# Storing the first of four output units in four column pieces instead of one DMA

## Chip, cores, metric

One core of a Trainium2 chip. The metric is the device time of one execution in microseconds (us), median of several runs. The profile's span is about 1.75 us shorter than that time (82.8 for 84.5).

## The reference, cut to what matters

Rotary embedding on an array of 8 x 8 heads, 1024 positions, 64 columns, single precision: 16.8 MB in, 16.8 MB out.

```
angles = np.outer(positions * scale, freqs)
cos, sin = np.cos(angles), np.sin(angles)
out_first  = x_first * cos - x_second * sin
out_second = x_first * sin + x_second * cos
```

## The kernel before

The array is cut into four units of 128 partitions x 8192 columns (4 MB in single precision, 32 KB per row). GpSimd issues the loads of units 1 to 3, which cast to half precision on the way. VectorE computes each half of a unit, ScalarE copies it to a single-precision output buffer. The kernel before stores units 0 and 1 whole, from GpSimd's queue; units 2 and 3 go out in halves, from SyncE's queue.

```
xout = ctx.enter_context(tc.tile_pool(name="xout", bufs=3))
...
pin(nc.gpsimd.dma_start(out=Xf[0][:, :NH], in_=xv[0][:, :NH]))
...
for u in range(1, NU):
    pin(nc.gpsimd.dma_start(out=Xf[u], in_=xv[u]))
...                                     # tables of sine and cosine: cut
for u in range(NU):
    OUT = xout.tile([P, N], FP32, tag="O")
    for s in range(2):
        ...                             # four VectorE instructions: cut
        pin(nc.scalar.copy(out=OUT[:, ns], in_=Xf[u][:, ns]))
        if u >= NU // 2:
            pin(nc.sync.dma_start(out=ov[u][:, ns], in_=OUT[:, ns]))
    if u < NU // 2:
        pin(nc.gpsimd.dma_start(out=ov[u], in_=OUT))
```

Of the kernel before, what the change touches and what calls it, by code (L numbers as in the profile page):

```python
# [21 lines left out]
def kernel(  # L22
# [8 lines left out]
    nc = tc.nc  # L31
    pin = tc.keep_in_program_order
# [8 lines left out]
    N = K * D  # L41
# [11 lines left out]
    ov = out.rearrange("b h s d -> (b h s d)").rearrange("(u p n) -> u p n", p=P, n=N)  # L53
# [34 lines left out]
        out=one, in_=one, compare_op=ALU.not_equal, fill=1.0, base=0,  # L88
        pattern=[[-1, G], [-G, HP]], channel_multiplier=1,
    ))  # L90
    for u in range(1, NU):
# [9 lines left out]
        out=posf, in_=pos_i64.bitcast(I32).rearrange("p (k t) -> p k t", t=2)[:, :, 0]  # L101
# [3 lines left out]
        out=y,  # L105
# [8 lines left out]
        out=r, in0=m, scalar=_MAGIC, in1=y, op0=ALU.subtract, op1=ALU.subtract  # L114
# [5 lines left out]
        out=ra.bitcast(I32), in0=r.bitcast(I32), scalar1=0x7FFFFFFF, scalar2=None, op0=ALU.bitwise_and  # L120
# [5 lines left out]
    for g in range(0, G, 2):  # L126
        ps = spread.tile([P, 2, 2, W], FP32, tag="g")
        for i in range(2):
            nc.tensor.matmul(  # L129
                out=ps[:, i].rearrange("p t w -> p (t w)"),  # L130
# [12 lines left out]
# [3 lines that stand above are left out]
            ks = slice(s * KH, (s + 1) * KH)  # L146
            ns = slice(s * NH, (s + 1) * NH)
            Xs = X[u][:, ks]
            sin_b = T[:, 0, ks].unsqueeze(2).broadcast_to((P, KH, 2, half))
            cos_b = T[:, 1, ks].unsqueeze(2).broadcast_to((P, KH, 2, half))  # L150
            pr = tmp.tile([P, KH, 2, half], FP16, tag="pr")
            pin(nc.vector.tensor_tensor(out=pr, in0=Xs, in1=sin_b, op=ALU.mult))  # L152
            pin(nc.vector.tensor_tensor(out=Xs, in0=Xs, in1=cos_b, op=ALU.mult))  # L153
            pin(nc.vector.tensor_tensor(  # L154
                out=Xs[:, :, 0, :], in0=Xs[:, :, 0, :], in1=pr[:, :, 1, :], op=ALU.subtract
            ))
            pin(nc.vector.tensor_tensor(  # L157
                out=Xs[:, :, 1, :], in0=pr[:, :, 0, :], in1=Xs[:, :, 1, :], op=ALU.add
            ))
            pin(nc.scalar.copy(out=OUT[:, ns], in_=Xf[u][:, ns]))  # L160
            if u >= NU // 2:
                pin(nc.sync.dma_start(out=ov[u][:, ns], in_=OUT[:, ns]))
        if u < NU // 2:
            pin(nc.gpsimd.dma_start(out=ov[u], in_=OUT))  # L164


# [33 lines left out]
```

## Time and profile before

| | before |
|---|---|
| time, median (range) | 84.51 us (84.47 to 84.59) |
| span of the profile | 82.8 us |
| VectorE busy | 60.3 us (73%) |
| ScalarE busy | 40.1 us (49%) |
| HBM traffic | 33.6 MB, 406 GB/s over the span |

The page's part on DMA queues (columns: packets, MB, share of 16 engines' span) says how the traffic is split. q0 is GpSimd's queue, q1 SyncE's, q10 ScalarE's:

```profile
q0 software_dynamic: 864, 15.73, 66.4%
q1 hardware_dynamic: 720, 9.44, 27.2%
```

The shares of the queues (with 3.2% for q10) add to 97%: the 16 DMA engines have work nearly all the time. VectorE at 73% works early and stops 13 us before the end. The prediction reads the rows that show this. Beside the views, it and this document use the trace's record of single DMA packets (start, queue, bytes, duration); tables of those are in ordinary fences. A packet is one stretch of work of one of the 16 engines. Every large DMA ends on each engine with a completion packet of 4 bytes; the DMA has landed when the semaphore that it counts up is full. The period of packets is the time from one start to the next on one engine, and a ring is what one queue has in store for one engine. The record doesn't name the engine, so periods rest on linking each packet to the one that starts where it ends.

### The profile page before, as it was taken

The numbers are of one execution on the slowest core, as the hardware profiler recorded it, in microseconds if no ns is written. First come the engines' busy times: TensorE is split into PE (matmuls) and PEld (weight loads), VectorE is DVE, ScalarE is ACT, GpSimd is POOL, SyncE is SP. The second block draws the span as 40 slices with busy tenths as digits, with TensorE's granted clock in tenths as the row PEclk, the third lists the DMA queues.
The fourth block names the chain that finished last, engine by engine and source line by source line (L and its number), as shares of the span: only waits on it lengthen the run. The fifth ranks groups of instructions, "written<-read, shape, count | busy, mean of one in ns | idle before, by whom it ended". The sixth has DMA issues, their size and how long they took to land.

```text
span 82.8 us, 179 instructions
## 1 busy us (share of the span) xinstructions
PE 7.0 (8%) x18; PEld 2.7 (3%) x18; DVE 60.3 (73%) x40; ACT 40.1 (49%) x18; POOL 4.6 (6%) x14
## 2 busy tenths in 40 slices
PE   0011799200000000000000000000000000000000
PEld 0011233000000000000000000000000000000000
DVE  0306276999999999999999999999999997000000
ACT  0602159999960690294088049209606912950000
POOL 4920000000000002000000200000000000000000
PEclk9999999975555555555555555555555555555555
DMA  2899998997999899699979989999899999999991
GB/s 40 335 326 269 293 333 182 253 238 150 246 253 198 182 253 238 143 253 253 127 301 459 507 348 412 507 443 420 380 436 420 412 420 436 444 420 436 428 428 55
DMA packets 1874, 26.22 MB, mean 317 GB/s; under 512 B 338, under 2 KB 338, under 8 KB 338
## 3 DMA queue, kind: packets, MB, share of 16 engines
q0 software_dynamic: 864, 15.73, 66.4%
q1 hardware_dynamic: 720, 9.44, 27.2%
q10 hardware_dynamic: 290, 1.06, 3.2%
HBM read 16.79 MB, written 16.78 MB: 406 GB/s over the span
## 4 chain that ended last, share of the span: by engine, by line
DVE 55%; ACT 14%; issue 6%; DMA 6%; PE 5%; DVEq 1%; ACTq 0%
DVE pr L152 19%; DVE X L153 19%; DVE X L157 9%; DVE X L154 6%; DMA freq_row<-in_freqs_dram 6%; ACT T L139 5%; ACT OUT L160 4%; PE ps L129 4%; ACT X L140 4%; DVEq L195 1%; PE cfreq L97 1%; ACT tab L122 1%; DVE r L113 1%; DVE y L104 1%; ACTq L69 0%
## 5 line engine op out<-in xcount | busy, mean ns | idle before, releaser
L160 ACT CAST OUT<-X 128x4096 f32<-128x4096 f16 x8 | 28.8, 3606 | 24.2 <-DVE X L157 24.2
L152 DVE TENSOR_TENSOR pr<-X,T 128x4096 f16<-128x4096 f16 x8 | 18.3, 2292 | 1.0 <-ACT T L139 0.7
L153 DVE TENSOR_TENSOR X<-X,T 128x4096 f16<-128x4096 f16 x8 | 18.3, 2292 | 0.3
L154 DVE TENSOR_TENSOR X<-X,pr 128x2048 f16<-128x2048 f16 x8 | 9.8, 1225 | 0.3
L157 DVE TENSOR_TENSOR X<-pr,X 128x2048 f16<-128x2048 f16 x8 | 9.7, 1219 | 0.0
L139 ACT CAST T<-ps 128x1024 f16<-128x1024 f32 x6 | 5.7, 1030 | 2.6 <-PE ps L129 2.6
L129 PE MATMUL ps<-tab,sel 128*128 128x512 f16 x16 | 6.4, 584 | 2.2 <-ACT tab L122 2.2
L137 DVE CAST T<-ps 128x1024 f16<-128x1024 f32 x2 | 2.5, 1225 | 2.2 <-PE ps L129 2.2
L140 ACT CAST X<-X0f 128x4096 f16<-128x4096 f32 x1 | 3.7, 3651 | 0.0
L164 POOL DMA_DIRECT2D out_dram<-OUT x2 | 1.1, 536 | 40.3 <-ACT OUT L160 40.3
L95 DVE COPY sel<-one 128x2048 f16<-128x2048 f16 x1 | 0.7, 693 | 2.8 <-POOL one L87 2.8
L117 ACT ACTIVATE tab<-r 128x256 f16<-128x256 f32 x1 | 0.4, 416 | 4.3 <-DVE r L113 4.3
L129 PEld LDWEIGHTS <-sel 128*128 128x128 f16 x16 | 2.2, 138 | 6.0 <-issue 5.8
L117 ACT ACT_TABLE_LOAD x1 | 1.3, 1283 | 2.1 <-issue 2.1
L92 POOL DMA_DIRECT2D X<-in_x_dram x3 | 2.0, 658 | 0.0
L100 DVE CAST posf<-pos_i 128x8 f32<-128x8 int32 x1 | 0.2, 172 | 2.3 <-DMA pos_i<-in_positions_dram 2.3
L97 PE MATMUL cfreq<-freq_row,coef 1*128 1x32 f32 x2 | 0.6, 392 | 5.9 <-DMA freq_row<-in_freqs_dram 5.9
L104 DVE TENSOR_TENSOR y<-posf,cfreq 128x256 f32<-128x256 f32 x1 | 0.4, 422 | 0.5 <-PE cfreq L97 0.5
L83 POOL DMA_DIRECT2D X<-in_x_dram x1 | 0.7, 667 | 0.8 <-POOLq L181 0.8
L97 PEld LDWEIGHTS cfreq<-freq_row,coef 1*128 1x128 f32 x2 | 0.5, 305 | 5.8 <-issue 5.8
L122 ACT ACTIVATE tab<-ra,quarter 128x256 f16<-128x256 f32 x1 | 0.5, 507 | 0.0
L113 DVE SCALAR_TENSOR_TENSOR r<-m,y 128x256 f32<-128x256 f32 x1 | 0.4, 424 | 0.0
(10 smaller groups left out, 1.9 us busy)
## 6 DMA issues: line engine op xcount, KB each, us to landing
out_dram<-OUT POOLq DMA_DIRECT2D x2, 4096.0 KB, 20.8
out_dram<-OUT SPq DMA_DIRECT2D x4, 2048.0 KB, 11.6
X<-in_x_dram POOLq DMA_DIRECT2D x3, 2048.0 KB, 28.7
X0f<-in_x_dram SPq DMA_DIRECT2D x1, 1024.0 KB, 4.8
X<-in_x_dram POOLq DMA_DIRECT2D x1, 1024.0 KB, 11.7
X0f<-in_x_dram ACTq DMA_DIRECT2D x1, 1024.0 KB, 12.2
pos_i<-in_positions_dram ACTq DMA_DIRECT2D x1, 8.0 KB, 5.0
freq_row<-in_freqs_dram ACTq DMA_DIRECT2D x1, 0.1 KB
```

The lines of the kernel that those rows point to most:

```text
L92: pin(nc.gpsimd.dma_start(out=Xf[u], in_=xv[u]))
L97: nc.tensor.matmul(out=cfreq, lhsT=coef, rhs=freq_row, start=True, stop=True)
L117: pin(nc.scalar.activation(out=tab[:, 0], in_=r, func=AF.Sin, bias=0.0, scale=-_TWO_PI_DN))
L129: nc.tensor.matmul(out=ps[:, i].rearrange("p t w -> p (t w)"), lhsT=sel[:, g + i].rearrange("s h q -> s (h q)"), rhs=tab.rearrange("s t k ...
L137: pin(nc.vector.tensor_copy(out=dst, in_=ps))
L139: pin(nc.scalar.copy(out=dst, in_=ps))
L140: pin(nc.scalar.copy(out=Xf[0][:, NH:], in_=X0f[:, :NH]))
L152: pin(nc.vector.tensor_tensor(out=pr, in0=Xs, in1=sin_b, op=ALU.mult))
L153: pin(nc.vector.tensor_tensor(out=Xs, in0=Xs, in1=cos_b, op=ALU.mult))
L154: pin(nc.vector.tensor_tensor(out=Xs[:, :, 0, :], in0=Xs[:, :, 0, :], in1=pr[:, :, 1, :], op=ALU.subtract))
L157: pin(nc.vector.tensor_tensor(out=Xs[:, :, 1, :], in0=pr[:, :, 0, :], in1=Xs[:, :, 1, :], op=ALU.add))
L160: pin(nc.scalar.copy(out=OUT[:, ns], in_=Xf[u][:, ns]))
```

## The change

Unit 0 is stored in four DMAs of 2048 columns (1 MB each, rows of 8 KB). As the quarters lie within one half each, the first two can be issued as soon as the first half is ready. The intent is to start the first store earlier, in smaller pieces.

```diff
         if u < NU // 2:
-            pin(nc.gpsimd.dma_start(out=ov[u], in_=OUT))
+            parts = 4 if u == 0 else 1
+            for i in range(parts):
+                c = slice(i * N // parts, (i + 1) * N // parts)
+                pin(nc.gpsimd.dma_start(out=ov[u][:, c], in_=OUT[:, c]))
```

## The prediction

> **What bounds the kernel now.** I read the page's slices first, then the table of DMA issues, then a table of stretches, and last the chain.
>
> The row of slices (each slice is 82.8 / 40 = 2.07 us):
>
> ```profile
> DVE  0306276999999999999999999999999997000000
> ACT  0602159999960690294088049209606912950000
> POOL 4920000000000002000000200000000000000000
> ...
> DMA  2899998997999899699979989999899999999991
> ...
> HBM read 16.79 MB, written 16.78 MB: 406 GB/s over the span
> ```
>
> VectorE is full from slice 7 to slice 33 and then stops; the DMA row is full from slice 2 to slice 39 and is still full in the five or six slices in which no engine computes. That is the first sign that the data movement sets the end. The stretches make it firm (columns: stretch, its length, busy time and count of PE, PEld, DVE, ACT, POOL, the granted clock, the DMA share, GB/s):
>
> ```profile
> 32.00:42.00 10.00, 0.00 (x0) 0.00 (x0) 9.83 (x8) 3.95 (x2) 0.06 (x1) 0.50 0.95 184
> 42.00:52.00 10.00, 0.00 (x0) 0.00 (x0) 9.86 (x6) 6.56 (x2) 0.53 (x1) 0.50 1.02 439
> 52.00:62.00 10.00, 0.00 (x0) 0.00 (x0) 9.86 (x7) 3.92 (x2) 0.00 (x0) 0.50 1.00 431
> 62.00:72.00 10.00, 0.00 (x0) 0.00 (x0) 7.71 (x5) 5.76 (x2) 0.00 (x0) 0.50 0.99 423
> 72.00:80.00 8.00, 0.00 (x0) 0.00 (x0) 0.00 (x0) 1.45 (x1) 0.00 (x0) 0.50 1.00 428
> ```
>
> The DMA share is 0.95 to 1.02 in each stretch. The rate jumps at 42 us because loads cast to half precision and the view counts the bytes that arrive: 184 GB/s of half precision is 368 GB/s read in this stretch. After 42 us it is stores alone, near 430 GB/s to the end.
>
> Third, when each store is issued and lands (KB each, us from issue to landing; the first two lines come from views of the stretches around each issue, the third from the one around the last store):
>
> ```profile
> out_dram<-OUT POOLq DMA_DIRECT2D x1, 4096.0 KB, 21.2
> ...
> out_dram<-OUT POOLq DMA_DIRECT2D x1, 4096.0 KB, 20.4
> ...
> out_dram<-OUT SPq DMA_DIRECT2D x1, 2048.0 KB, 8.4
> ```
>
> Unit 0's store is issued at 31.52 us and lands 21.2 us later, at 52.7. The trace's record of single DMA packets shows its first packet at 42.05 us: it spends 10.5 us waiting behind the loads, which share GpSimd's queue (q0), and 9.7 us moving. The last store, from SyncE, is issued at 73.45 and lands 8.4 us later, though it holds 2 MB, which takes 4.86 us to move (first packet 76.36, completion packets from 80.87 on). So it too queues, for nearly 3 us, behind stores issued before it.
>
> The chain of waits must be read against this. It says
>
> ```profile
> DVE 55%; ACT 14%; issue 6%; DMA 6%; PE 5%; DVEq 1%; ACTq 0%
> ```
>
> and ends with the last ScalarE copy (69.84 to 73.44 us). It follows semaphores and doesn't see transfers queue behind each other. From 42 us on the engines have work without a pause, so any DMA time added to unit 0's store moves every later packet and the end.
>
> **What the Trainium skill says.** (1) "DMA: Bandwidth & Descriptors", section "Why small descriptors are slow (HBM only)": each packet carries a fixed overhead of about 3 cycles on the engine's inner bus, against 32 bytes per cycle of data. The trace agrees in size, see below. (2) The same page, "Anatomy of one DMA", puts a fixed cost near 2.0 us on each DMA, mostly completion latency. The trace shows that such latency isn't paid by the next DMA in the queue: on one engine the completion packet of unit 0's store starts at 51.734 us and the first data packet of unit 1's at 51.740. (3) "Queues, rings and completion order": an engine takes descriptors in ring order and goes round the queues packet by packet. The trace agrees: unit 0's store begins only when the third load is through (its completion packets at 42.04 to 42.67 us), and when SyncE's first store joins unit 1's, 16 KB and 32 KB packets alternate with a period of 1.816 us, the sum of one of each.
>
> **The change part by part.**
>
> *Issue.* The order of instructions shows that GpSimd's four quarters no longer all wait for both ScalarE copies: the first two need only the first (ends at 24.0 us), the last two the second (31.2 us). Four issues at 0.54 us each cost GpSimd 4 x 0.54 = 2.1 us in place of 0.54; it has nothing else to do there (it waited 26.8 us before this store). So half of the unit is issued some 7 us earlier. It brings nothing: the ring is in order, and the third load fills it until 42 us in either case.
>
> *Data packets.* A row of unit 0 is now four packets of 8 KB in place of one of 32 KB. I take the period from one packet's start to the next on one engine:
> - 32 KB, unit 0's store alone: 1209.5 ns (median).
> - 16 KB, the last stores, alone: 607 ns.
> - A straight line through both: 1209.5 - 607 = 602.5 ns for 16 KB, so 301.25 ns for 8 KB, and 607 - 602.5 = 4.5 ns fixed per packet. An 8 KB packet should take 305.75 ns.
> - Check: the first load has 8 KB packets, with a 64-byte packet of the positions between them; period 313 ns, the small packet takes 7 ns of it, so 306 ns. (The skill's 3 cycles, at 32 bytes per cycle and 27.1 bytes per ns, i.e. 32768 / 1209.5, are an estimate of 3.5 ns: the same size.)
>
> Per row: 4 x 305.75 - 1209.5 = 13.5 ns. Each engine has 128 / 16 = 8 rows: 8 x 13.5 = 0.108 us.
>
> *Completion packets.* Three DMAs more, each with one completion packet per engine. They are recorded with 9 ns and set the next data packet back by 6: 3 x 6 to 9 = 0.02 to 0.03 us.
>
> *Waits.* Unit 3's first output copy reuses unit 0's buffer and must now wait for four stores. It starts at 62.84 us, released by VectorE; unit 0's store lands at 52.7 and would land at 52.8. 10 us of slack, so nothing. Unit 1's store (45.56 us) gets a wait on a semaphore reused from the first load, which landed before 13 us: nothing.
>
> *VectorE, ScalarE.* No instruction is changed. VectorE has about 2 us of slack before the last store would come late to its engines (issued at 73.45, first packet 76.36; the first load shows about 1.0 us from issue to first packet).
>
> Sum: 0.11 + 0.02 = 0.13 us on the DMA engines, all of it passed to the end because they are full until 81.5 us. 84.51 + 0.13 = 84.64 us, or +0.15%.
>
> **The rivals.**
>
> *A fixed cost per DMA is paid in series.* If each of three added DMAs cost the skill's 2.0 us, the time would be 84.5 + 6 = 90.5 us. Against it speak the 6 ns between two DMAs of one ring above, and the same at the load-to-store boundary.
>
> *An earlier start pays.* If quarters issued at 24 us could slip in between the loads, or if the first half landed early, it would matter only if it freed work or filled idle DMA time. The DMA share has no hole between 5 and 81 us, and the loads it would displace would be late by as much. Worth 0 to -0.3 us; and a later load might then stop VectorE: unit 3's data lands at 43 us and is needed at 55.75, so 12 us of slack hides even that.
>
> *Descriptor writing on GpSimd is slow beside VectorE, or the ring fills.* GpSimd's four issues fall beside VectorE's 2.3 us multiplies. The before shows 0.53 to 0.54 us for each such issue beside VectorE, so no sign of a clash; even a doubling ends before 35 us, 7 us ahead of need. A ring too small for 3 more sets of descriptors would hold GpSimd up until loads drain, and this could leave a hole at 42 us. Nothing shows a limit; if it struck I would expect under 1 us.
>
> *Shorter HBM runs cost more.* Each quarter writes 8 KB at a pitch of 32 KB. SyncE's stores already write 16 KB at that pitch at the full rate (607 ns); the first load reads 8 KB at it, also full. For writes of 8 KB there is no direct evidence. At a 5% loss: 0.05 x 9.7 = 0.5 us, 85.0 us.
>
> **Range and chances.** The three timed runs before span 84.47 to 84.59, so the effect is about the size of their spread. Downward I allow 0.15 us of noise or a better joint between loads and stores, upward 0.3 us for the HBM and ring rivals: 84.4 to 84.9. Leaving the 2% band needs 1.7 us, over ten times my sum; only the first or third rival, which the trace speaks against, gives it. Within 2%: 0.96; slower 0.025; faster 0.015.
>
> **What the profile after would show.** q0 has 3 x 128 = 384 data packets more and 3 x 16 = 48 completion packets more, so 864 + 432 = 1296 packets and the same 15.73 MB. 8 KB store packets run at about 306 ns from 42.05 us to about 51.87 (before: 51.74). GpSimd's issues start near 24 and 31.5 us. The last landing moves from 81.86 to about 82.0 us, and VectorE and ScalarE keep their starts within 0.1 us. The prediction is wrong if 8 KB packets are longer than 320 ns, if there is a pause between the quarters, if store packets show up before the loads end, or if the end doesn't follow the DMA engines.

## The result, and the profile after

84.69 us median (84.53 to 84.73, six runs) against 84.51 (six runs). The ratio is 1.0016 with a 95% interval of 1.0003 to 1.0029: slower, and clear of noise, by 0.03% to 0.29%. Ratios here are the mean time of one kernel's runs over that of the other's of the same rounds, so not quite the ratio of the quoted medians. A second set of six runs (below) gave 1.0025. The prediction was 84.64 us, with a range of 84.4 to 84.9.

The page's slices of the kernel after (tenths busy in 40 slices), then its line of q0:

```profile
DVE  0306376999999999999999999999999995000000
...
POOL 4920000000031005000001100000000000000000
...
DMA  2899997997999799799969999989999899999990
```

```profile
q0 software_dynamic: 1296, 15.73, 66.5%
```

GpSimd now has issues in slices 12 and 13, 7 us ahead of the ones in slice 16, but the DMA row is as full as before and of the same shape. q0 has 1296 packets in place of 864 for the same bytes, and its share of the engines' time grew by 0.1% of the span.

GpSimd's timeline of the kernel after (start, us, engine, line, operation, count, idle time before and what ended it), and where its transfers land (from views of the stretches around each issue; KB each, us from issue to landing):

```profile
24.11 1.08 POOL L167 DMA_DIRECT2D out_dram<-OUT  x2 [19.45 <-ACT OUT L160]
31.33 1.05 POOL L167 DMA_DIRECT2D out_dram<-OUT  x2 [6.13 <-ACT OUT L160]
45.37 0.53 POOL L167 DMA_DIRECT2D out_dram<-OUT  x1 [12.98 <-ACT OUT L160]
```

```profile
out_dram<-OUT POOLq DMA_DIRECT2D x2, 1024.0 KB, 22.4
...
out_dram<-OUT POOLq DMA_DIRECT2D x2, 1024.0 KB, 20.1
...
out_dram<-OUT POOLq DMA_DIRECT2D x1, 4096.0 KB, 20.9
...
out_dram<-OUT SPq DMA_DIRECT2D x1, 2048.0 KB, 8.7
```

The first two quarters are issued at 24.11 us and need 22.4 us (median) to land; the last two are issued 7 us later and need 20.1. The early start became queueing. The last store takes 8.7 us in place of 8.4.

The stretches of the kernel after (columns as in the prediction):

```profile
32.00:42.00 10.00, 0.00 (x0) 0.00 (x0) 9.84 (x7) 4.14 (x2) 0.38 (x1) 0.50 0.96 184
42.00:52.00 10.00, 0.00 (x0) 0.00 (x0) 9.86 (x6) 6.56 (x2) 0.53 (x1) 0.50 1.00 421
...
72.00:80.00 8.00, 0.00 (x0) 0.00 (x0) 0.00 (x0) 1.26 (x1) 0.00 (x0) 0.50 1.00 430
```

The DMA share stays at 0.96 to 1.00. The 421 GB/s against 439 of before in the second line must not be read as a slower store: a packet is counted whole at its start, and before, six packets of 32 KB of unit 1 started in the last 0.3 us ahead of 52 us. Packet records don't have that edge. For them I take the mean, over the 16 engines, of the time at which a transfer's completion packet starts:

```
                        third load done   unit 0 stored   difference
before                       42.39            52.09           9.69 us
after                        42.41            52.24           9.82 us
after, run again             42.40            52.22           9.82 us
```

(The differences here and below are taken before rounding.)

The store takes 0.13 us more of each engine, as forecast. The last landing moves from 81.86 to 82.02 us and the span from 82.76 to 82.92.

### The profile page after: what moved, and what is told of

Same layout as the page of the kernel before. It is cut to its first block, busy times and chain, and to the rows that moved or that the text cites. A ratio compares the mean times of both kernels' runs of the same rounds, so it can differ in the third digit from the quotient of the medians.

```text
span 82.9 us, 185 instructions
## 1 busy us (share of the span) xinstructions
PE 6.5 (8%) x18; PEld 2.6 (3%) x18; DVE 60.3 (73%) x40; ACT 40.1 (48%) x18; POOL 6.2 (7%) x17
## 3 DMA queue, kind: packets, MB, share of 16 engines
q0 software_dynamic: 1296, 15.73, 66.5%
## 4 chain that ended last, share of the span: by engine, by line
DVE 55%; ACT 15%; DMA 5%; issue 5%; PE 5%; DVEq 1%; ACTq 0%
DVE pr L152 19%; DVE X L153 19%; DVE X L157 9%; DVE X L154 6%; ACT T L139 6%; DMA freq_row<-in_freqs_dram 5%; ACT OUT L160 4%; PE ps L129 4%; ACT X L140 4%; DVEq L198 1%; PE cfreq L97 1%; ACT tab L122 1%; DVE r L113 1%; DVE y L104 1%; ACTq L69 0%
## 5 line engine op out<-in xcount | busy, mean ns | idle before, releaser
L129 PE MATMUL ps<-tab,sel 128*128 128x512 f16 x16 | 5.9, 536 | 2.5 <-ACT tab L122 2.2
L167 POOL DMA_DIRECT2D out_dram<-OUT x5 | 2.7, 538 | 38.6 <-ACT OUT L160 38.6
## 6 DMA issues: line engine op xcount, KB each, us to landing
out_dram<-OUT POOLq DMA_DIRECT2D x1, 4096.0 KB, 20.9
```

What stands on the lines that cost most here:

```text
L129: nc.tensor.matmul(out=ps[:, i].rearrange("p t w -> p (t w)"), lhsT=sel[:, g + i].rearrange("s h q -> s (h q)"), rhs=tab.rearrange("s t k ...
L167: pin(nc.gpsimd.dma_start(out=ov[u][:, c], in_=OUT[:, c]))
```

## The experiments

My theory: the engines are full from 42 us to the end, so what unit 0's store costs them moves the end one for one; the cost is a fixed time per packet (0.11 us in all) and the completion packets of three more DMAs (0.02 us); the earlier issue is worth nothing behind the loads. The rivals: the cost belongs to the DMAs, not the packets; the earlier issue hides part of it; compute sets the end. Eleven other kernels were run, and the changed one again. The diffs are against the changed kernel where they show `parts` or a slice `c`, else against the kernel before; cuts in them are marked. The DMA times of those that keep unit 0 on GpSimd's queue are in one table, as above:

```
                        third load done   unit 0 stored   difference
late_quarters                42.44            52.27           9.82 us
four_by_rows                 42.30            58.90          16.60 us
two_dmas_2k                  42.40            52.57          10.16 us
sixteen_by_columns           42.36            52.51          10.15 us
two_dmas_512b                42.10            55.50          13.40 us
drop_1024                    42.33            50.82           8.49 us
```

### late_quarters: the same quarters, none of them early

```diff
-            for i in range(parts):
+            for i in reversed(range(parts)):
```

> The same four quarters, issued last quarter first, so that the first one issued waits for both ScalarE copies and all four are issued from about 31.3 us on, none at 24 us. My theory (the ring holds every store back until the loads are through at 42 us, so the early issue is worth nothing): the same as the changed kernel, 84.65 us within 0.1, first 8 KB store packet at 42.1 us, 32 packets per engine in 9.82 us. Rival (the early issue gains something that hides part of the packets' cost): slower than the changed kernel, 84.8 us or more.

GpSimd's timeline in this kernel:

```profile
31.36 2.12 POOL L167 DMA_DIRECT2D out_dram<-OUT  x4 [26.69 <-ACT OUT L160]
```

All four are issued from 31.36 us. Time 84.64 us, ratio to before 1.0015 (the changed kernel: 1.0016), the store 9.82 us of each engine in both. Starting the issue 7 us earlier is worth nothing that these runs resolve: the rival, which expected 84.8 us or more, falls.

### two_dmas_2k and sixteen_by_columns: smaller packets, few and many DMAs

The first stores the even 2 KB pieces of each row in one DMA and the odd ones in another; the second uses sixteen DMAs of 512 columns.

```diff
+            if u == 0:                  # other units as before: cut
+                for b in range(2):
+                    o = ov[u].rearrange("p (a b c) -> p b a c", b=2, c=512)[:, b]
+                    i = OUT.rearrange("p (a b c) -> p b a c", b=2, c=512)[:, b]
+                    pin(nc.gpsimd.dma_start(out=o, in_=i))
```
```diff
-            parts = 4 if u == 0 else 1
+            parts = 16 if u == 0 else 1
```

> Unit 0 in two DMAs, one of the even 2 KB pieces of each row and one of the odd ones: 16 packets of 2 KB per row, only one DMA more. From the straight line of the prediction (37.66 ns per KB and 4.5 ns per packet): a 2 KB packet 79.8 ns, a row 16 x 79.8 = 1277 ns, 67.5 ns over the 1209.5 of before, 8 rows 0.54 us, one completion packet 0.01: 0.55 us, 85.06 us. Rival (the cost goes with the number of DMAs): 84.51 + 0.13/3 = 84.55 us. Rival (short writes to HBM cost more than a fixed time per packet): over 85.3 us.

> Unit 0 in sixteen DMAs of 512 columns: the same 2 KB packets, fifteen DMAs more. There are eight semaphores for GpSimd's DMAs, so from the eighth piece on each issue waits for an older DMA to land (the eighth for the third load at 42.5 us). My theory: packets 0.54 us as in the run with two DMAs, completion packets 15 x 6 ns = 0.09 us, and the queue of seven pieces (4.2 us of work) hides the new waits: 0.63 us, 85.14 us. Rival 1 (each DMA pays a fixed latency that isn't hidden): several us more. Rival 2 (the new waits leave the engines idle around 43 to 50 us): holes in the DMA row there, over 86 us.

Measured: 85.08 us (ratio 1.0074, 1.0061 to 1.0087) and 85.00 us (1.0053, 1.0040 to 1.0067). The page's line of q0 in the run with two DMAs, then in the one with sixteen:

```profile
q0 software_dynamic: 1776, 15.73, 66.7%
```

```profile
q0 software_dynamic: 2000, 15.73, 66.7%
```

Each count reads as follows. Before, unit 0 is 128 data packets and 16 completion packets of 864. With two DMAs, 864 - 128 - 16 + 2 x 16 = 752 packets without unit 0's data, and 1776 - 752 = 1024 for it: packets of 4 KB, two 2 KB pieces each, not the 2048 that I assumed. With sixteen DMAs, 864 - 144 + 16 x 16 = 976 and again 1024. The two kernels therefore differ in the number of DMAs (2 and 16) and in the order of their pieces.

The stores take 10.16 and 10.15 us. Fourteen more DMAs cost nothing that shows in these totals, and smaller packets cost 0.46 us: the cost lies with the packets, not with the DMAs. Both packets have a median period of 156.0 ns, where the straight line gives 4 x 37.66 + 4.5 = 155.1. The completion packets are hidden in the pair rather than free. With sixteen DMAs one of them takes 0.627 us of an engine against 4 x 156 = 624 ns, so about 3 ns for its completion packet and 0.04 us for fourteen; the run with two DMAs has as much and more in slow packets (its mean period is 158.8 ns, since about a hundred of its 1024 packets, from 48 us on, are longer; why is not known).

My sum for two_dmas_2k was 0.55 us; the packet record gives 0.47 (10.16 - 9.69) and the timed runs 0.63 (0.0074 x 84.5). That the total came near is luck: with half as many packets as assumed, the same line gives only 8 x (8 x 155.1 - 1209.5) = 251 ns, or 0.25 us, and the rest is the longer mean period.

GpSimd's timeline with sixteen DMAs shows the new waits:

```profile
24.26 3.20 POOL L167 DMA_DIRECT2D out_dram<-OUT  x6 [19.58 <-ACT OUT L160]
32.58 0.54 POOL L167 DMA_DIRECT2D out_dram<-OUT  x1 [5.11 <-DMA X<-in_x_dram]
43.34 0.54 POOL L167 DMA_DIRECT2D out_dram<-OUT  x1 [10.23 <-DMA X<-in_x_dram]
44.36 4.64 POOL L167 DMA_DIRECT2D out_dram<-OUT  x8 [0.47 <-issue]
49.38 0.54 POOL L167 DMA_DIRECT2D out_dram<-OUT  x1 [0.39 <-issue]
```

The eighth piece waits 10.23 us for the third load to land, because its semaphore is that load's. The seven pieces issued before hold some 4 us of work, so the engines don't see it. With four pieces no such wait arises; whether still more pieces would leave the engines empty, no run here shows.

### two_dmas_512b: the straight line pushed further

```diff
-                    o = ov[u].rearrange("p (a b c) -> p b a c", b=2, c=512)[:, b]
+                    o = ov[u].rearrange("p (a b c) -> p b a c", b=2, c=128)[:, b]
```
(and the same for the source; this diff is against two_dmas_2k.)

> Unit 0 in two DMAs of 512-byte pieces, even and odd: 64 packets per row. From the straight line: a packet 18.83 + 4.5 = 23.3 ns, a row 64 x 23.3 = 1493 ns, 284 more than before, 8 rows 2.27 us: 86.8 us. Rival (the number of DMAs costs): 84.55 us. Rival (below some size the cost per packet grows, or writing 512 descriptors per engine holds GpSimd up so long that the engines run dry): 87.5 us or more, and in the second case a hole in the DMA row near 42 us.

88.86 us, ratio 1.0510: 4.3 us more than before, where I had summed 2.27 and set 87.5 as the mark for the rival that cost per packet grows. The records again show packets of 4 KB, now of eight pieces, and they have no one period. Of 1024, 45% last 159 to 174 ns, most of them 174, a period of 171: (171 - 150.6) / 8 = 2.5 ns a piece, where 150.6 ns is the line's time for 4 KB of data alone. The others last 181 ns and more (median 231), the first of them from 44.2 us on. The mean period is 13.40 us / 64 = 209 ns, or 7.3 ns a piece. So there is a cost per piece, and the quicker packets stay below my line (8 x 171 = 1368 ns a row against 1493); what broke the sum is a slowing in the course of the store. Its cause is open: the first slow packets come before GpSimd issues its next store at 45.45 us, and no run isolates it. The store takes 13.40 us, 3.7 more than before, and the 16 engines' last landings now lie 2.0 us apart (84.27 to 86.27) in place of 0.66, which the end waits out. The first form of the rival, a price that grows, is thus what the time shows, with the mark of 87.5 passed. The second form is not seen; in the stretches of this kernel the share stays full:

```profile
42.00:52.00 10.00, 0.00 (x0) 0.00 (x0) 9.86 (x6) 6.56 (x2) 0.55 (x1) 0.50 1.01 322
```

A full share at 322 GB/s means that the packets take longer, not that the engines wait for work. A straight line taken from 16 and 32 KB packets holds at 8 KB (306 ns), holds for the median packet of two 2 KB pieces but not for their sum (0.47 us against 0.25), and fails for the store in 512-byte pieces.

### four_by_rows: three more DMAs with the packets of before

```diff
-                c = slice(i * N // parts, (i + 1) * N // parts)
-                pin(nc.gpsimd.dma_start(out=ov[u][:, c], in_=OUT[:, c]))
+                c = slice(i * P // parts, (i + 1) * P // parts)
+                pin(nc.gpsimd.dma_start(out=ov[u][c, :], in_=OUT[c, :]))
```

> Four DMAs of 32 partitions each with whole rows of 32 KB: three DMAs more than before, the packets of before. My theory (0.11 us of the 0.13 is the fixed cost of packets, 0.02 is completion packets): unit 0's store takes 9.69 + 0.02 = 9.71 us per engine, and the time is 84.53 us, not told from before. Rival 1 (the cost lies in the number of DMAs): the time of the changed kernel, 84.65, and a store of 9.82 us per engine. Rival 2 (32 partitions reach fewer of SBUF's ports and the packets slow down): packets clearly over 1213 ns, store 10 us or more, 84.8 us or more.

97.67 us, ratio 1.157. This was meant to isolate the number of DMAs and doesn't: two other things happen. First, many packets of 32 KB now take about 2550 ns in place of 1213, and the store 16.60 us. The Trainium skill, "SBUF — State Buffer", section "Door 1: The DMA port swizzle", says that 32 neighbouring partitions reach 8 of 16 ports; a doubled packet time fits that, but the record doesn't bear it out as the whole reason. The first of the four DMAs holds 32 partitions too, and all its packets take 1226 or 1213 ns (1 MB in 2.44 us); only the three behind it are slow, at 4.40, 4.53 and 5.24 us. No run here isolates the ports, so the cause stays open. Second, the waits of this kernel show

```profile
POOL out_dram L167 <- ACT OUT L160: 38.8, 2, 26.7
ACT OUT L160 <- DMA out_dram<-OUT: 20.9, 1, 20.9
```

ScalarE waits 20.9 us for a store. In the built program, unit 3's output copy here waits for unit 2's two stores, not for unit 0's: the pool handed it another buffer than in the other kernels. The table of stretches has the outcome, a DMA share (column before the last) of 0.59 in a stretch in which the kernels before and after are full:

```profile
62.00:72.00 10.00, 0.00 (x0) 0.00 (x0) 7.61 (x5) 0.00 (x0) 0.00 (x0) 0.50 1.04 446
72.00:82.00 10.00, 0.00 (x0) 0.00 (x0) 0.00 (x0) 1.82 (x1) 0.00 (x0) 0.50 0.59 252
```

So the run says nothing on the price of three DMAs; the pair above answers that.

### drop_1024 and drop_unit0: is the end really set by DMA time?

Both give a wrong result: the last 1024 columns of unit 0, or all of it, are never stored.

```diff
-            pin(nc.gpsimd.dma_start(out=ov[u], in_=OUT))
+            n = N - 1024 if u == 0 else N
+            pin(nc.gpsimd.dma_start(out=ov[u][:, :n], in_=OUT[:, :n]))
```
```diff
-            pin(nc.gpsimd.dma_start(out=ov[u], in_=OUT))
+            if u > 0:
+                pin(nc.gpsimd.dma_start(out=ov[u], in_=OUT))
```

> Wrong result on purpose: unit 0 in one DMA without its last 1024 columns, so 28 KB in place of 32 KB per row. My theory (the DMA engines are full from 42 us to the end, so DMA time of unit 0 moves the end one for one): an eighth of 9.68 us is 1.21 us, so 83.30 us. Rival (VectorE and ScalarE set the end, as the chain of waits says): 84.51 us, no change.

> Wrong result on purpose: unit 0 is not stored at all, 9.7 us of DMA time less. My theory: the queue in front of the last store vanishes, and the end is then set by the last ScalarE copy (73.44 us): issue, about 1.0 us to the first packet, 4.86 us of packets, the same tail. First packet near 74.5 in place of 76.36, so 1.9 us less, 82.6 us; that is the slack of the compute chain against the DMA engines. Rival (VectorE and ScalarE set the end already): 84.51 us.

drop_1024: 83.26 us, ratio 0.9846 (0.9833 to 0.9859) to before, so 1.30 us less (1.19 to 1.41); the store takes 9.69 - 8.49 = 1.20 us less of each engine. One for one within the interval, and the compute rival, which expects no change, falls.

drop_unit0: 82.30 us, ratio 0.9732, 2.27 us less where I expected 1.9 (from the 76.36 us that the last part corrects). Of 9.7 us taken away only these show, since compute then sets the end. Its timeline and the stretch after the loads:

```profile
73.27 0.33 SPq L162 DMA_DIRECT2D out_dram<-OUT  x1
```

```profile
42.00:52.00 10.00, 0.00 (x0) 0.00 (x0) 9.86 (x6) 6.56 (x2) 0.54 (x1) 0.50 0.61 262
```

The share drops to 0.61 where before it was 1.02: the engines now run dry while they wait for the next store. The last store is issued at 73.27 us and its first packets start at 74.10 to 74.25 on all 16 engines, 0.83 to 0.98 us after issue (I had assumed 1.0). So about 2.3 us is how far compute runs ahead of the DMA engines in the kernel before (in this trace 0.2 us of it is a last store issued at 73.27 in place of 73.47 us), and a store that cost them 0.13 us more is paid in full.

### quarters_on_sync, whole_on_sync, halves_on_sync, all_halves_on_sync: off the loads' queue

If the ring makes unit 0's store wait behind the loads, SyncE's queue would let it mix with them.

```diff
+                q = nc.sync if u == 0 else nc.gpsimd          # quarters_on_sync
-                pin(nc.gpsimd.dma_start(out=ov[u][:, c], in_=OUT[:, c]))
+                pin(q.dma_start(out=ov[u][:, c], in_=OUT[:, c]))
```
```diff
+            q = nc.sync if u == 0 else nc.gpsimd              # whole_on_sync
-            pin(nc.gpsimd.dma_start(out=ov[u], in_=OUT))
+            pin(q.dma_start(out=ov[u], in_=OUT))
```
```diff
-            if u >= NU // 2:
+            if u != 1:                  # halves_on_sync; all_halves_on_sync: if True
...
-        if u < NU // 2:
+        if u == 1:                      # halves_on_sync; all_halves_on_sync: gone
```

> The four quarters are issued by SyncE, on another queue than the loads. My theory (order doesn't matter as long as the engines are full): store packets of 8 KB start near 25 us and alternate with the loads' packets, the third load lands near 47 us in place of 43 and is still ahead of its need at 55.6 us; the sum of the work is the same, 84.64 us within 0.15. Rival 1 (an early start pays): 84.3 us or less. Rival 2 (mixing reads and writes costs, or VectorE is held up by a late load): 85 us or more.

84.33 us (84.29 to 84.44), ratio to before 0.9974 (0.9960 to 0.9987): 0.22 us less than before in spite of the 8 KB packets, and the fastest correct kernel. By the ratios to before it is 0.42% to 0.51% faster than the changed kernel, from which it differs in the issuer alone. The third load lands at 46.3 us (43.0 before) and VectorE isn't late. "Order doesn't matter", with 84.64 expected, was wrong by 0.3 us. For the reason I looked at the packets where loads and stores meet. In the kernel before, the second load completes at 31.73 us and the third at 42.39, 10.66 us apart, where the one ahead took 9.69. In drop_unit0, which has no store behind the third load, it is 9.68 again. About 1.0 us is lost at that joint; the last load packets there are recorded with 1.8 to 2.2 us in place of 1.23. I took the saving of that loss as the reason and made three more kernels:

> Unit 0 in one DMA with 32 KB rows as before, but issued by SyncE on the other queue, at 31.5 us. In the kernel before, the third load completes 10.66 us after the second, where the load before took 9.69 us, so about 1.0 us is lost where the loads end and the first store begins behind them in one ring; with the quarters on SyncE 0.64 us was lost from the second load to the end of unit 2's first half. My theory (that joint is what SyncE's queue saves, about 0.35 us, and the quarters give back 0.13 of it): 84.15 to 84.25 us. Rival (the gain of the quarters on SyncE came from starting at 24 us, which this kernel doesn't): 84.4 to 84.55 us.

> Unit 0 in two DMAs with 16 KB rows on SyncE's queue, the first at 24 us, the second at 31.3 us. My theory: the saving of SyncE's queue with 0.04 us of packet cost: 84.2 to 84.3 us. Rival (the early start is what pays): clearly below the run with the whole unit on SyncE, by 0.15 us or more.

> All four units are stored in halves from SyncE; GpSimd's queue holds loads alone, so no store lies behind a load in one ring. My theory (the loss is at the one joint of unit 0, which is gone already): 84.2 to 84.35 us, as with the halves of unit 0. Rival (each meeting of two queues costs): below the halves of unit 0 by 0.2 us or more, since the queues then meet only while the loads last.

All three are slower than before, not faster:

```
                     time us  ratio to before    last landing  span us  landing to end  semaphores checked
before                84.51                          81.86      82.76       0.90               1
quarters_on_sync      84.33   0.9974                 81.53      82.67       1.14               5
whole_on_sync         84.87   1.0072                 81.64      82.96       1.32               8
halves_on_sync        84.73   1.0029                 81.76      83.02       1.26               7
all_halves_on_sync    84.65   1.0019                 81.74      82.88       1.14               5
```

(95% intervals of the last three: 1.0035 to 1.0109, 1.0017 to 1.0041, 1.0007 to 1.0032; two of whole_on_sync's six runs, 85.36 and 85.84, are unlike the other four, which end at 84.89.) My expectations fail in time, for all three. The trace splits the failure in two. All four kernels have their last landing earlier than before, by 0.10 to 0.33 us. That is one trace each, and the times of before alone spread over 0.25 us in one set of rounds, so the 0.10 and 0.12 of the two kernels in halves show no saving on the engines; whole_on_sync has 0.21 in place of the 0.35 I had put down. And then more is lost at the very end, which repeats far better (0.89 to 0.90 us in before, after and after_again). The program has SyncE check the DMA semaphores one after another, in a fixed order, 0.061 us each. Before, the last store's semaphore stands last in that order and one check is left when it lands; with more DMAs on SyncE's queue the last store gets an earlier semaphore and four to seven further checks come after it: 0.90 + 7 x 0.061 = 1.32 us, and so for the others. SyncE's waits show it as two waits or one. Of the kernel before:

```profile
SPq L195 <- DMA out_dram<-OUT: 7.6, 2, 4.8
```

Of whole_on_sync:

```profile
SPq L196 <- DMA out_dram<-OUT: 8.0, 1, 8.0
```

Before, SyncE waits twice, for the store before the last and for the last; with the whole unit on its queue it waits once, on the last store's semaphore at the head of the order, and has all others still to check. This is read from the traces; no run changed the order alone. Nor does it set the quarters apart: all_halves_on_sync has the same 1.14 us at the end and is still 0.45% slower by the ratios.

What stays open is why a store behind a load in one ring loses 1.0 us, and why quarters save more than halves or the whole (from the completion of unit 1's load, near 22.0 us, to that of unit 2's first half, the losses against the sum of undisturbed times are 0.97 us before, 0.60 for the quarters, 0.77 for halves, 0.70 for all units in halves, 0.84 for the whole). So most of the loss remains when the store isn't behind the loads in their ring. Neither of my two reasons, the joint alone or the early start alone, gives this order. An estimate, not run: the quarters on SyncE with the last store on the semaphore checked last would save 4 x 0.061 = 0.24 us more, 84.1 us.

### after_again

> The changed kernel once more, for the same chip and the same rounds: 84.65 us within 0.08, 0.13 us over before.

84.64 us (six runs), ratio to before 1.0025 (1.0012 to 1.0037), 0.19 us between the medians. With the first set (1.0016) and late_quarters (1.0015) the timed cost is 0.13 to 0.21 us; the packet records say 0.13.

## Why the prediction was right, point by point

*The bound.* Right: drop_1024 moves the end by what it takes off the engines. The prediction has two slips here. It counts five or six full slices in which no engine computes; ScalarE copies until 73.44 us, in slice 36, so only 37 to 39 are such. And it gives 76.36 us as the first packet of the last store. That is the time at which the store ahead of it began to land, and the mean over the engines; the first packet starts at 76.01 us. From the issue at 73.47 that is 2.5 us, not nearly 3, of which about 0.8 would pass without a queue (drop_unit0). Nothing in the sum rests on either.

*The issue.* Right: issues at 24.1 and 31.3 us, and late_quarters shows that the earlier two are worth nothing.

*Data packets.* Right in size and in kind. Forecast 305.75 ns for 8 KB and 0.108 us in all; the records show a median period of 306 ns, and 9.82 - 9.69 = 0.13 us with the completion packets. The number of DMAs does not carry the cost (two_dmas_2k and sixteen_by_columns). Whether the fixed time belongs to each packet or to each piece in it, the prediction could not tell apart, as its pieces and packets were the same: packets of 4 KB carry 5.4 ns over their data with two pieces and 20.4 with eight (the quicker ones), so the pieces have a price of their own.

*Completion packets.* A forecast of 0.02 to 0.03 us, below what the timed runs resolve; the records fit 3 ns (sixteen_by_columns) to 5 ns (2.453 us for a quarter against 8 x 306 ns) each, so 0.01 to 0.02 us.

*Waits.* Right: no new wait of ScalarE, and unit 1's store is issued at 45.37 us (45.56 before).

*VectorE and ScalarE.* I said that their starts would stay within 0.1 us. They came 0.19 us earlier (first VectorE multiply at 13.17 in place of 13.36), because the row of frequencies landed at 5.54 in place of 5.73 us, long before the change. Compute ran 0.19 us ahead and the end still came 0.16 us later, one more sign that compute doesn't set it. Its slack, "about 2 us", is 2.3 by drop_unit0; as the sum behind it used 76.36 us (76.01 would have given 1.5), that it came near is partly luck.

*The rivals.* A serial cost per DMA, a brake by descriptor writing and a full ring do not appear at four or at sixteen DMAs. "An earlier start pays" doesn't hold on this queue; on SyncE's queue, which the prediction didn't consider, quarters do gain. Writes of 8 KB at a pitch of 32 KB cost no more than the fixed time.

*Sum.* 84.64 us forecast, 84.69 and 84.64 measured in two sets.

## What to carry to other kernels

Before moving a store earlier, ask what stands ahead of it in its queue and whether the DMA engines have a hole to take it; with full engines behind a queue of loads, an early issue only lengthens the wait. Price a split in packet periods read from the trace of the kernel itself, and check the price by making the suspected term larger, with the other one held, rather than by repeating a run for a tenth of a per cent. When an experiment moves a DMA to another queue, look at the last microsecond as well: the order of the final semaphore checks can take back what the transfers saved.

## What the Trainium skill lacked or had wrong

To the page "DMA: Bandwidth & Descriptors" belong the first four points:

- Section "SWDGE vs HWDGE vs iDMA": a packet is said to be at most 4096 bytes by preference. A row of 32 KB is one packet here (1213 ns), and queues alternate at that size (1.816 us for a pair of 32 and 16 KB). Pieces of 2 KB and 512 bytes do go out as packets of 4 KB.
- Section "Why small descriptors are slow (HBM only)": 3 cycles per packet, an estimate of 3.5 ns, against 4.5 ns measured; right in kind. It says that packing small pieces into one packet leaves a second cost, 32 bytes of metadata for each, but gives no time for it. With eight 512-byte pieces to a packet 2.5 ns a piece are lost in the quicker packets and 7.3 on average.
- Section "Anatomy of one DMA": it calls the fixed 2.0 us mostly completion latency and the write to the semaphore itself nearly free, but doesn't say that the next DMA of the same ring doesn't pay the latency: 6 ns between two of them, and the store of unit 0 takes 10.15 us in sixteen DMAs and 10.16 in two.
- Section "Issuing engines are not separate DMA queues": moving a DMA to another issuer is said to save only issue time. The quarters on SyncE's queue gained 0.26% over the kernel before (interval 0.13% to 0.40%), and the last landing moved by 0.33 us. One kernel of four: the other three moves to SyncE's queue gained no time.

On no page:

- About 1.0 us is lost where a store follows a load in one ring (10.66 us against 9.69 between completions); with the store on another queue 0.60 to 0.84 us are lost over the same work.
- At the end of this program SyncE checks the DMA semaphores one by one, 0.061 us each, and the place of the last store's semaphore in that order was worth up to 0.42 us by the traces.
